# Means of squares as pairs of float32r products, some slots behind the lead group, in a two-block transformer on one core

## The chip, the core and the metric

The kernel runs on one core of one Trainium2 chip, in one launch. The metric is device time in microseconds (us): the median over executions on the chip. One execution was taken by the hardware profiler, and all rows below are from it. The engines are named as the profile names them: PE (matrix products; PEld is its loading of weights), DVE (vector), ACT (scalar functions), POOL, and SP, which here only issues transfers.

## What is computed

The input is one sequence of 512 tokens of width 1024. All arithmetic is to float32's accuracy. The first block has two layers, the second block one layer with a state space operator and one with attention:

```python
def rmsnorm(x, g):
    xf = x.astype(jnp.float32)
    y = xf * lax.rsqrt(jnp.mean(xf * xf, axis=-1, keepdims=True) + EPS)
    return (y * g.astype(jnp.float32)).astype(x.dtype)
...
    for l in range(DEPTH):
        u = rmsnorm(x, pre_mix_g[l])
        m = token_mixer(u, w_in[l], b_gate[l], q_norm_g[l], k_norm_g[l],
...
        x = x + rmsnorm(m, post_mix_g[l])
        h = rmsnorm(x, pre_ffn_g[l]) @ w_ffn_up[l]
        f = jnp.square(jax.nn.relu(h)) @ w_ffn_down[l]
        x = x + rmsnorm(f, post_ffn_g[l])
...
        h = rms_norm(x, norm_mix[layer])
        if layer < N_A_LAYERS:
            x = x + s5_mixer(h, ssm_w_in[layer], ssm_a_re[layer], ssm_a_im[layer],
...
        x = x + conv_ffn(rms_norm(x, norm_ffn[layer]), ffn_w_up[layer],
```

In `token_mixer` the product with `w_in` gives queries, keys and values of a grouped-query attention, a query and a key of lower rank (the latents; each gets an rmsnorm of its own before it is multiplied up), and gates. The change is about the means of squares inside these norms: those of the stages' inputs and those of the latents.

## The kernel before

**Layout.** Activations lie feature-major: 1024 features are 8 tiles of 128 partitions by 512 tokens. Each weight and each activation is kept as a pair of float32r parts, hi and lo, and each product is made in three float32r passes (hi by hi, hi by lo, lo by hi). In the trace such a triple is two rows `mm<-xg,wh` and one row `mm<-xg,wl`. An output tile of a product over 8 tiles of input is 24 products of 512 columns. A product of plain float32 operands is two records in the trace.

**The norm is applied late.** A stage multiplies the input, scaled by the norm's gain, with its weights at once, and the factor 1/sqrt(mean + eps) of each token is applied when an output tile leaves PSUM. So the mean of squares must be known only then. The squares are made by ACT (`sq`), summed over the 8 tiles by POOL and DVE (`acc`; in most stages the last tile's square stays apart in `sq`), and `mean_mm` sums over the partitions with one or two float32 products by a matrix of 1/n (`ones_d` in the tile `consts`). `rstd` then makes the factor `rr` with Ln, Exp and Square on ACT and two steps on DVE.

**The lead group.** A stage begins with `lead_group`: its first three or four output tiles are made input tile by input tile, so that PE can start with the first input tile. Inside a boundary between stages it does so for the two halves of the columns one after the other, while DVE and ACT make the input tiles `xg`. Behind its last product stands `pre()`, which is the mean and `rstd`, and four slots later the closures that take the group's tiles out of PSUM. There are 8 PSUM tiles.

**Order.** The program is a list of closures. `later(n, fn)` puts a closure behind n more slots of products, where a slot is 512 columns of float32r, and a float32 product of 512 columns counts as four. The scheduler of the framework then orders the instructions of each engine by its own estimate of times; `pin` keeps an instruction behind what its engine was given before. So a stage's closures can move when another closure's products count otherwise.

**The state space stage** (`ssm`). PE makes `u` tiles as any stage; DVE applies the factor (`u<-mm,rr`), and each tile goes out to DRAM (`ud`) and comes back in another order (`U`). Blocks of eight float32 products of at most 64 columns follow: `vps<-U` (the chunk's contribution to the states, copied by ACT into `VS0`, `VS1`, `VS2`, which hold tiles 0 and 1, tiles 2 to 4 and tiles 5 to 7), `yps<-U`, `yps<-VS` and `yps<-fx`. Between them DVE runs a scan over each of VS0, VS1 and VS2 (lines 1427 to 1431, five operations a step), in the order of the program. In the profile's rows the number is left out, so that VS0 and VS1 both read VS. The result, after `gq`, comes back as `yhl`, and the products `mm<-yhl` with the stage's second weight follow.

Of the kernel before, what the change touches and what calls it, by code (L numbers as in the profile page):

```python
# [107 lines left out]
class Kernel:  # L108
# [21 lines left out]
    LAG = 3  # L130
    LD = 2
# [28 lines left out]
    # ---------------------------------------------------------------- tiles  # L160
# [20 lines left out]
    # -------------------------------------------------------------- weights  # L181
# [14 lines left out]
    def split_early(self, h):  # L196
        """half of the first three units"""
        for u in self.early:
            t = self.raw[u][0]
            if h == 0:  # L200
                hi, lo = (self.pool.tile([128, 1024], F32R, name=x, tag=x, bufs=W_BUFS) for x in ("wh", "wl"))
                self.whl[u] = [hi], [lo], 1024
            c = slice(512 * h, 512 * h + 512)
            hi, lo = self.whl[u][0][0][:, c], self.whl[u][1][0][:, c]
            self.pin(self.nc.scalar.activation(hi, t[:, c], AF.Copy))
            self.nc.vector.tensor_tensor(lo, t[:, c], hi.bitcast(F32), ALU.subtract)
            if h == 1:
                self.raw.pop(u)
# [29 lines left out]
    def weight(self, u, a, m):  # L238
        """columns a .. a + m of both parts of a unit"""
# [53 lines left out]
    def later(self, n, fn):  # L293
        """emit fn once n more slots (of 512 columns) of products have been emitted"""
# [11 lines left out]
    # ------------------------------------------------------------- matmuls  # L306
# [7 lines left out]
    def pin(self, ins):  # L314
        """ins stays behind what its engine has been given so far"""
        self.tc.keep_in_program_order(ins)

    def mm_tok(self, out, x, t, u, a, first, last, n=256):
        """out [128 tokens of tile t, n] += x[:, tokens].T @ W[columns a .. a + n of a unit], in three float32r passes"""
# [14 lines left out]
    def mm3(self, ps, u, k0, nk, kt, m0, m, xs, first, last, ncol=None, cols=ALL):  # L334
        """ps += W[k-tiles, cols].T @ x over nk k-tiles, in three float32r passes."""
# [10 lines left out]
    def split(self, dst, src, scale=None, gain=None):  # L346
        """dst[:,0] + dst[:,1] = src (times scale or a per-partition gain)."""
# [14 lines left out]
    def ln(self, out, in_, load=True, **kw):  # L362
        """Ln from the table set that has Exp too; load: unless it is there already."""
# [6 lines left out]
    def rstd_a(self, v, l=None, cols=ALL, load=True):  # L370
        """v: mean square, the same in all the rows it is used for (PSUM)."""
# [8 lines left out]
    def rstd_b(self, vyq, name="r", cols=ALL, r=None, pin=False):  # L380
        """one Newton step; the result is -2 / sqrt(v + eps): y * ((v + eps) * y * y - 3)"""
# [12 lines left out]
    # ------------------------------------------------------- generic phases  # L394
    def sq_acc(self, st, src, i, n, scale=1.0, cols=ALL, pin=False, one=False):
        """running sum of squares over tiles; the last stays apart."""
# [26 lines left out]

    def lead_group(self, units, n, xs, evac, st, ones="ones_d", pre=None, mid=None, feed=None):
        """The first n output tiles k-tile by k-tile, so that the products start with the first tile of x;
        mid: the two halves of the columns one after the other, with mid() once the first has begun."""
        pss = []

        def emit(k, cols, last):
# [4 lines left out]
            if last and k == KT - 1:  # L434
                if pre is not None:
                    pre()
                    self.later(4, lambda: [evac(j, pss[j]) for j in range(n)])
# [34 lines left out]
    def half_tiles(self, units, xs, nk, evac, js, fin):  # L472
        """the last output tiles, the two halves of the columns one after the other; fin() in the second"""
# [24 lines left out]
    # ================================================================ setup  # L498
# [37 lines left out]
    def begin_norm(self, gain, xs, st):  # L536
        """split x * gain, and start the sum of squares of x: a closure for each tile."""
# [8 lines left out]
    def boundary(self, f, st, gain, nxt, res):  # L546
        """x += the norm of f; then begin_norm of the next norm; the closures for the two halves of the columns."""
# [29 lines left out]
    # ================================================================= FFN  # L577
    def ffn1(self, l, xs, st, nxt, mid, bg=None, last=(), feed=None):
# [7 lines left out]
        def pre():  # L586
            st["r"] = self.rstd(self.mean_mm(st, self.const("ones_d")), "rr", load=False)
# [55 lines left out]
    # =============================================================== mixer  # L643
# [9 lines left out]
    def head_norm(self, z, gain, then, n1, n2):  # L653
        """rms norm over the 64 rows of each head, times gain; then(result)."""
# [17 lines left out]
    def v_tiles(self, vf, vst):  # L672
        """v feature-major [two heads of 64, tokens] -> vst [token, tile, head, (hi | lo)]."""
# [8 lines left out]
    def stack(self, dst, src, scale=None):  # L682
        """src [two heads of 64, S] -> dst[h] with hi and lo stacked on the partitions."""
# [11 lines left out]
    def dup(self, dst, src, scale=None):  # L695
        """src [two heads of 64, S] -> dst[h] [128, (hi, lo), S], each on both halves of the partitions."""
# [13 lines left out]
    def softmax_ops(self, name, qk, vst, ydst, spill=None):  # L710
        """The parts of a softmax attention over 8 heads in blocks of 128 queries, by name; a block (h, qt) is 4 h + qt.
        q: scores, e: exponentials, n: division by the sum, t: transposes, p: product with the values, two blocks at once.
        qk(h, qt, ps): scores. vst(h): [128, 4, 128] (hi | lo). ydst: pairs of heads -> hi/lo tiles."""
# [69 lines left out]
    def chunks(self, unit, xs, nk, evac, j, n, m0=0, ncol=None, k0=0):  # L783
        """one output tile as n closures, for use between other work."""
# [14 lines left out]
    def mixer(self, l, xs, st, nxt, mid, feed=None):  # L799
# [6 lines left out]
        def pre():  # L806
            st["r"] = self.rstd(self.mean_mm(st, self.const("ones_d")), "rr", load=False)
# [59 lines left out]
        def ev_c(which, n):  # L867
            def f(j, ps):
# [3 lines left out]
                if j == n - 1:  # L872
                    self.later(18, mean)

            def mean():
                a = self.rstd_a(self.mean_mm(cst[which], self.const("ones_" + which)))
# [16 lines left out]
        def kr_mm():  # L893
            """the products of both parts of w_kr with hi in one pass, one below the other"""
# [26 lines left out]
        # ---- grouped-query attention  # L921
# [8 lines left out]
        # ---- latent attention operands, a pair of heads at a time  # L930
# [36 lines left out]
        def v_chunk(i, c):  # L967
            """the values of the heads of two pairs, for two tiles of tokens, token-major"""
# [16 lines left out]
        def prep(p):  # L985
# [5 lines left out]
            # column tiles of q_up: rope0 nope0 | nope1 rope1 | nope2 nope3  # L991
# [64 lines left out]
        # ---- branches, gates and output product  # L1056
# [48 lines left out]
    # ======================================================== second block  # L1105
    def exp32(self, x, n, out):
        """exp to float32's accuracy on a small tile: 2^k * polynomial."""
# [58 lines left out]
    def ssm_gen(self):  # L1166
        """The state space operators, from the parameters alone, as a list of closures:
        WT (chunk -> state), O (state -> chunk) and T (the lags inside a chunk) in DRAM.
        States have the real part on the first 64 partitions, the imaginary on the others;
        the places j of a chunk are stored from the last to the first."""  # L1170
# [33 lines left out]
        def factor():  # L1204
            """f = (a_bar - 1) / a"""
# [20 lines left out]
        def powers(R, I, n):  # L1226
            """the powers n + 1 .. 2n from 1 .. n"""
# [15 lines left out]
        def tables():  # L1243
            """P1 = re | im, P2 = -im | re of the powers 0 .. 8"""
# [7 lines left out]
        def outer():  # L1252
            """powers 1 .. 8 of a_bar^8 for the scan"""
# [13 lines left out]
        def expansion(out, c1, c2, a):  # L1267
            """out[g, d, h] = c1[g, h] * P1[a + d, g] + c2[g, h] * P2[a + d, g]; in closures"""
# [19 lines left out]
        def gen(i):  # L1288
# [10 lines left out]
            def bbar():  # L1299
                """bb = f * b"""  # L1300
# [12 lines left out]
            def stacks():  # L1313
                """bs = bb re | bb im, c = c | -c, c0 = c re | -c im"""
# [60 lines left out]
    def ssm(self, xs, st, nxt, mid, feed=None):  # L1375
# [9 lines left out]
        def pre():  # L1385
            st["r"] = self.rstd(self.mean_mm(st, self.const("ones_d")), "rr", load=False)
# [28 lines left out]
        def scan(k):  # L1415
            """states after each chunk: inside blocks of 8 chunks, from block to block, and the blocks' starts added."""
# [6 lines left out]
            def step(s, o, m, sh, temp):  # L1423
                """o += a * s, with a = m(re) and m(im | -im)"""
# [632 lines left out]
```

## Time and profile before

| what | value |
|---|---|
| device time, median of 3 runs | 2788.34 us (2786.98 to 2790.88) |
| span of the profiled execution | 2786.1 us |
| PE busy | 2722.6 us, 98% |
| DVE busy | 1846.5 us, 66% |
| ACT busy | 1305.1 us, 47% |
| POOL busy | 293.4 us, 11% |

The profiled execution's own time is its span and what lies around it; the median of the runs is 2.2 us above the span. PE is busy for nearly the whole span, so a PE instruction that is removed, or a wait of PE that is shortened, is what can be seen in the time; an instruction on another engine is seen only where PE waits for it.

### The profile page before, as it was taken

The page shows a single profiled execution, that of the slowest core. Times are in us where ns is not written, and L with a number is a line of the kernel's source. Part 1 is how long each engine was busy: PE and PEld are TensorE (multiplying, and loading weights), DVE is VectorE, ACT ScalarE, POOL GpSimd, SP SyncE. Part 2 cuts the span into 40 slices and gives each one's busy share as a digit, 9 for nine tenths or more (in the row PEclk, how much of TensorE's full clock was granted, in tenths as well). Part 3 has the DMA queues.
Part 4 walks back from the last instruction along what each step waited for, and adds up shares of the span by engine and source line. Part 5 has one row for each costly group of instructions (what it writes and reads, how often), then busy time and mean ns, then how long its engine had stood idle before and what let it go on. Part 6 is the DMA issues. An engine that isn't in the chain of part 4 may idle for free.

```text
span 2786.1 us, 35356 instructions
## 1 busy us (share of the span) xinstructions
PE 2722.6 (98%) x13470; PEld 2268.2 (81%) x13470; DVE 1846.5 (66%) x2963; ACT 1305.1 (47%) x2204; POOL 293.4 (11%) x311
## 2 busy tenths in 40 slices
PE   8999999999999999999999989999999999999998
PEld 6888888888878888888887887888887888888887
DVE  7889863444687996787745784656466667574654
ACT  6567553333465664532334214423236888542333
POOL 1000020000210101121002000101012111110101
PEclk9999999999999999999999879999999999999999
DMA  5323333333232334354445623233324223233331
GB/s 206 116 79 91 121 119 97 95 98 98 96 109 86 93 95 161 110 190 153 137 123 180 183 88 117 91 99 98 99 85 131 68 69 103 84 98 99 98 92 61
DMA packets 122651, 307.47 MB, mean 110 GB/s; under 512 B 35824, under 2 KB 42736, under 8 KB 122352
## 3 DMA queue, kind: packets, MB, share of 16 engines
q1 hardware_dynamic: 109424, 291.57, 32.7%
q10 hardware_dynamic: 10624, 8.39, 1.0%
q0 software_dynamic: 2432, 5.25, 0.9%
q8 instruction: 106, 1.74, 0.3%
q14 instruction: 65, 0.53, 0.1%
HBM read 260.59 MB, written 41.68 MB: 108 GB/s over the span
## 4 chain that ended last, share of the span: by engine, by line
PE 58%; DVE 5%; ACT 1%; issue 1%; DMA 0%; POOL 0%; SPq 0%; DVEq 0%; ACTq 0%; POOLq 0%
PE mm L312 49%; PE z L312 3%; PE yps L312 2%; PE o L312 1%; PE s L312 1%; PE vps L312 1%; DVE xg L360 0%; DVE wl L233 0%; PE gps L312 0%; PE pT L328 0%; DVE pn L567 0%; PE mean L312 0%; DVE xr L568 0%; DVE VS L1431 0%; PE gps L328 0%
## 5 line engine op out<-in xcount | busy, mean ns | idle before, releaser
L312 PE MATMUL mm<-xg,wh 128*128 128x512 f32 (+1 forms) x4080 | 1227.5, 383 | 26.6 <-DVE xg L360 15.5
L312 PEld LDWEIGHTS mm<-xg,wh 128*128 128x128 f32 x4080 | 745.4, 188 | 188.0 <-DVE xg L360 24.6
L230 ACT ACTIVATE wh<-raw 128x1024 fp32r<-128x1024 f32 (+2 forms) x417 | 431.1, 1039 | 830.0 <-PE mm L312 527.5
L312 PE MATMUL mm<-xg,wl 128*128 128x512 f32 (+1 forms) x2024 | 759.5, 378 | 0.0
L233 DVE TENSOR_TENSOR wl<-raw,wh 128x1024 fp32r<-128x1024 f32 (+2 forms) x417 | 531.3, 1278 | 161.9 <-ACT wh L230 156.7
L312 PE MATMUL mm<-hid,wh 128*128 128x512 f32 (+1 forms) x1816 | 539.1, 380 | 0.7 <-DVE hid L357 0.4
L312 PEld LDWEIGHTS mm<-xg,wl 128*128 128x128 f32 x2024 | 381.7, 189 | 71.6 <-issue 0.2
L312 PEld LDWEIGHTS mm<-hid,wh 128*128 128x128 f32 x1816 | 335.0, 188 | 67.0 <-DVE hid L357 1.2
L312 PE MATMUL mm<-hid,wl 128*128 128x512 f32 (+1 forms) x908 | 343.9, 379 | 0.0
L312 PE MATMUL mm<-yhl,wh 128*128 128x512 f32 x640 | 207.3, 403 | 8.7 <-ACT yhl L1494 4.7
L414 POOL TENSOR_TENSOR acc<-acc,sq 128x256 f32<-128x256 f32 (+1 forms) x90 | 106.6, 1185 | 953.1 <-ACT sq L402 952.5
L312 PEld LDWEIGHTS mm<-hid,wl 128*128 128x128 f32 x908 | 170.8, 188 | 31.8
L312 PEld LDWEIGHTS mm<-yhl,wh 128*128 128x128 f32 x640 | 120.1, 192 | 34.6 <-DVE yhl L1495 5.7
L1582 POOL TENSOR_TENSOR gt<-gt,cv 128x512 f32<-128x512 f32 x44 | 74.9, 1703 | 592.7 <-ACT wh L230 471.1
L312 PE MATMUL mm<-yhl,wl 128*128 128x512 f32 x320 | 127.1, 397 | 0.0
L591 DVE SCALAR_TENSOR_TENSOR ht<-mm,rr 128x512 f32<-128x512 f32 x64 | 43.8, 690 | 117.1 <-PE mm L312 116.8
L1590 DVE SCALAR_TENSOR_TENSOR xr<-mm,xr 128x512 f32<-128x512 f32 (+1 forms) x50 | 33.5, 670 | 125.3 <-PE mm L312 125.3
L607 DVE TENSOR_TENSOR part<-part,mm 128x512 f32<-128x512 f32 (+1 forms) x52 | 33.5, 644 | 113.9 <-PE mm L312 113.8
L1570 DVE SCALAR_TENSOR_TENSOR gt<-mm,rr 128x512 f32<-128x512 f32 x88 | 60.6, 690 | 69.6 <-PE mm L312 69.5
L722 DVE TENSOR_REDUCE nm<-s 128x1 f32<-128x512 f32 x128 | 86.4, 680 | 20.8 <-PE s L312 20.4
L749 ACT ACTIVATE pt<-pT 128x512 fp32r<-128x512 f32 x128 | 74.6, 594 | 46.2 <-PE pT L328 45.0
L729 ACT ACTIVATE p<-s,nm 128x512 f32<-128x512 f32 x128 | 87.1, 684 | 11.0 <-DVE nm L722 8.9
(297 smaller groups left out, 3463.5 us busy)
## 6 DMA issues: line engine op xcount, KB each, us to landing
raw<-in_w_up SPq DMA_DIRECT2D x152, 512.0 KB, 3.6
raw<-in_w_down SPq DMA_DIRECT2D x96, 512.0 KB, 3.5
raw<-in_w_in SPq DMA_DIRECT2D x51, 512.0 KB, 3.6
xd<-xr SPq DMA_DIRECT2D x16, 512.0 KB, 2.8
gd<-z SPq DMA_DIRECT2D x32, 256.0 KB, 2.2
g<-gd SPq DMA_DIRECT2D x32, 256.0 KB, 3.9
raw<-in_w_o SPq DMA_DIRECT2D x16, 512.0 KB, 3.6
raw<-in_w_glu SPq DMA_DIRECT2D x16, 512.0 KB, 4.3
```

What stands on the lines that cost most here:

```text
L230: ins = self.nc.scalar.activation(h, x, AF.Copy)
L233: ins = lo_engine.tensor_tensor(l, x, h.bitcast(F32), ALU.subtract)
L312: return self.nc.tensor.matmul(out, lhsT, rhs, **kw)
L414: eng.tensor_tensor(st["acc"][:, cols], st["acc"][:, cols], sq[:, cols], ALU.add)
L591: nc.vector.scalar_tensor_tensor(t, ps, 0.0, st["r"], op0=ALU.max, op1=ALU.mult)
L607: nc.vector.tensor_tensor(p, p, ps[:, cols], ALU.add)
L722: nc.vector.tensor_reduce(nm, ps, AX.X, ALU.max, negate=True)
L729: nc.scalar.activation(p, ps, AF.Exp, bias=nm, accum_out=sm)
L749: nc.scalar.activation(hi[:, :, q0:q0 + 128], v, AF.Copy)
L1570: v.scalar_tensor_tensor(t, ps, -0.5, st["r"], op0=ALU.mult, op1=ALU.mult)
L1582: nc.gpsimd.tensor_tensor(t, t, sg.pop(n), ALU.mult)
L1590: v.scalar_tensor_tensor(x, ps[:, cols], 0.5, x, op0=ALU.mult, op1=ALU.add)
```

## The change

In seven lead groups (both mixers, both feed-forward stages of the first block, the state space stage, both feed-forward stages of the second block) and in the four norms of latents, the float32 products of `mean_mm` are replaced. `sum_split` makes one tile of the sum on DVE where the last square lay apart, and splits it, times -1/n, in a hi and a lo part (ACT and DVE, tile `mhl`); `mean_r` multiplies both parts by a float32r matrix of -1 that was there already. In the lead groups `pre()` moves 10 slots behind the group's last product (`PRE`), and the evacuation four slots behind that. In the latents the split stands 6 slots behind the last tile and the mean 18 slots behind it, as before. The attention stage of the second block, the boundaries, the head norms and the last norm keep float32. The rest of the diff takes out comments, so that line numbers behind line 130 move by 1, those behind line 430 by up to 19.

```diff
+    PRE = 10
...
+    def sum_split(self, st, n):
+        if "sq" in st:
+            self.nc.vector.tensor_tensor(st["acc"], st["acc"], st["sq"], ALU.add)
+        st["hl"] = self.s4("mhl")
+        self.split(st["hl"], st["acc"], scale=-1.0 / n)
+
+    def mean_r(self, st):
+        v = self.ps("mean")
+        for i in range(2):
+            self.mm(v, self.ones_r, st["hl"][:, i], start=i == 0, stop=i == 1)
+        return v
...
                 if pre is not None:
-                    pre()
-                    self.later(4, lambda: [evac(j, pss[j]) for j in range(n)])
+                    self.sum_split(st, D)
+
+                    def rest():
+                        pre()
+                        self.later(4, lambda: [evac(j, pss[j]) for j in range(n)])
+                    self.later(self.PRE, rest)
...
         def pre():
-            st["r"] = self.rstd(self.mean_mm(st, self.const("ones_d")), "rr", load=False)
+            st["r"] = self.rstd(self.mean_r(st), "rr", load=False)
...
                 if j == n - 1:
+                    self.later(6, lambda: self.sum_split(cst[which], 128 * n))
                     self.later(18, mean)
...
             def mean():
-                a = self.rstd_a(self.mean_mm(cst[which], self.const("ones_" + which)))
+                a = self.rstd_a(self.mean_r(cst[which]))
```

How the instructions move is not to be read from the diff. On PE, at the end of the first mixer's lead group (the first stage of the program), the order before is this; `xg` is the input, `wh` and `wl` the parts of the weights:

```order
L312 MATMUL mm<-xg,wl 128x512
L312 MATMUL mean<-acc,consts 128x512
L312 MATMUL mean<-sq,consts 128x512
L312 MATMUL mm<-xg,wh 128x512 x2
L312 MATMUL mm<-xg,wl 128x512
```

And with the change, from the same last product of the group on:

```order
L313 MATMUL mm<-xg,wl 128x512
L313 MATMUL mm<-xg,wh 128x512 x2
L313 MATMUL mm<-xg,wl 128x512
L313 MATMUL mm<-xg,wh 128x512 x2
L313 MATMUL mm<-xg,wl 128x512
L313 MATMUL mm<-xg,wh 128x512 x2
L313 MATMUL mm<-xg,wl 128x512
L313 MATMUL mm<-xg,wh 128x512 x2
L313 MATMUL mm<-xg,wl 128x512
L313 MATMUL mean<-mhl,ones_r 128x512 x2
L313 MATMUL mm<-xg,wh 128x512 x2
```

The mean stands 12 products later, since it is emitted between closures of 12 products, and is two float32r products instead of two float32 ones.

On PE in the state space stage, before the first products with the scanned states, the order before is:

```order
L312 MATMUL mm<-xg,wl 128x512
L312 MATMUL vps<-U,wt 128x64 x16
L312 MATMUL mm<-xg,wh 128x512 x2
L312 MATMUL mm<-xg,wl 128x512
L312 MATMUL mm<-xg,wh 128x512 x2
L312 MATMUL mm<-xg,wl 128x512
L312 MATMUL mm<-xg,wh 128x512 x2
L312 MATMUL mm<-xg,wl 128x512
L312 MATMUL yps<-VS_14466,ot 128x63 x8
L312 MATMUL vps<-U,wt 128x64 x8
L312 MATMUL yps<-fx,ot 128x7x7 x8
```

With the change it is as follows (VS_14466 before and VS_14502 here are both VS0):

```order
L313 MATMUL mm<-xg,wl 128x512
L313 MATMUL mm<-xg,wh 128x512 x2
L313 MATMUL mm<-xg,wl 128x512
L313 MATMUL yps<-VS_14502,ot 128x63
L313 MATMUL vps<-U,wt 128x64 x16
L313 MATMUL yps<-VS_14502,ot 128x63 x7
L313 MATMUL vps<-U,wt 128x64 x8
L313 MATMUL yps<-fx,ot 128x7x7 x8
```

The two blocks `vps<-U` of tiles 3 and 4, 16 products, stood ahead of the first product that needs the scanned VS0, and now stand behind it. From there on PE's order is the same as before to the end of the stage.

On DVE in the same stage, from the last input tile to the third `u`, the order before is:

```order
L360 SCALAR_TENSOR_TENSOR xg<-xr_13746,cols,xg 128x256 x2
L233 TENSOR_TENSOR wl<-raw,wh 128x1024 x2
L384 SCALAR_TENSOR_TENSOR rl<-mean,rl 128x512
L388 SCALAR_TENSOR_TENSOR rr<-rl,ry 128x512
L1390 SCALAR_TENSOR_TENSOR u<-mm,rr 128x512
L233 TENSOR_TENSOR wl<-raw,wh 128x1024
L1390 SCALAR_TENSOR_TENSOR u<-mm,rr 128x512
```

With the change:

```order
L361 SCALAR_TENSOR_TENSOR xg<-xr_13778,cols,xg 128x256 x2
L428 TENSOR_TENSOR acc<-acc,sq 128x512
L355 SCALAR_TENSOR_TENSOR mhl<-acc,mhl 128x512
L234 TENSOR_TENSOR wl<-raw,wh 128x1024 x3
L385 SCALAR_TENSOR_TENSOR rl<-mean,rl 128x512
L389 SCALAR_TENSOR_TENSOR rr<-rl,ry 128x512
L1409 SCALAR_TENSOR_TENSOR u<-mm,rr 128x512
```

Two operations of the split have come in, and a third weight (`wl`, which waits for ACT's `wh`) stands ahead of the chain that makes `rr`.

## Rows read from the trace of the kernel before

**Rows 1.** The page: span; busy time, share and instructions of PE.

```profile
span 2786.1 us, 35356 instructions
PE 2722.6 (98%) x13470; PEld 2268.2 (81%) x13470; DVE 1846.5 (66%) x2963; ACT 1305.1 (47%) x2204; POOL 293.4 (11%) x311
```

**Rows 2.** Timeline of PE, end of the lead group of the first feed-forward stage.

```profile
410.68 1.02 PE L312 MATMUL mean<-acc,consts 128*128 128x512 f32 x2
411.53 1.02 PE L312 MATMUL mean<-sq,consts 128*128 128x512 f32 x2
...
412.86 0.40 PE L312 MATMUL mm<-xg,wl 128*128 128x512 f32 x1
413.09 0.40 PE L312 MATMUL mm<-xg,wh 128*128 128x512 f32 x1
```

**Rows 3.** Timeline of PE, the first mean of a latent.

```profile
150.66 1.02 PE L312 MATMUL mean<-acc,consts 128*128 128x512 f32 x2
...
151.99 0.39 PE L312 MATMUL mm<-xg,wl 128*128 128x512 f32 x1
```

**Rows 4.** Timelines of DVE and ACT at the lead end of rows 2.

```profile
410.76 3.50 DVE L233 TENSOR_TENSOR wl<-raw,wh 128x1024 fp32r<-128x1024 f32 x3 [2.49 <-ACT wh L230]
...
409.67 2.95 ACT L230 ACTIVATE wh<-raw 128x1024 fp32r<-128x1024 f32 x3 [1.82 <-PE mm L312]
```

**Rows 5.** Instructions of lines 356 and 357: duration in ns, min/median/max.

```profile
L356 ACT ACTIVATE hid<-gt x44: 632/632/635, 1779.9 to 2742.2; 128x512 fp32r<-128x512 f32 x44
L357 DVE TENSOR_TENSOR hid<-gt,hid x44: 676/684/694, 1781.1 to 2742.8; 128x512 fp32r<-128x512 f32 x44
```

**Rows 6.** Timeline of PE inside the same lead group; in brackets the idle time before.

```profile
402.79 0.38 PE L312 MATMUL mm<-xg,wh 128*128 128x256 f32 x1 [0.81 <-DVE xg L360]
```

**Rows 7.** Timelines of PE and DVE, second mixer: its first scores.

```profile
809.94 1.16 PE L312 MATMUL s<-kk,qs 128*128 128x512 f32 x2 [5.26 <-DVE qs L693]
810.90 1.91 PE L312 MATMUL mean<-sq,consts 128*128 128x512 f32 x2
...
809.20 1.41 DVE L693 SCALAR_TENSOR_TENSOR qs<-qro,qs 64x512 fp32r<-64x512 f32 x2
```

**Rows 8.** Timeline of PE in the state space stage.

```profile
1577.97 3.76 PE L312 MATMUL vps<-U,wt 128*128 128x64 f32 x32 [0.67 <-DVE u L1390]
...
1587.07 2.60 PE L312 MATMUL yps<-VS,ot 128*128 128x63 f32 x16 [3.22 <-DVE VS L1431]
1589.46 3.62 PE L312 MATMUL vps<-U,wt 128*128 128x64 f32 x16
1592.88 3.60 PE L312 MATMUL yps<-fx,ot 128*128 128x49 f32 x16
...
1620.15 1.20 PE L312 MATMUL mm<-yhl,wh 128*128 128x512 f32 x2
...
1624.03 1.89 PE L312 MATMUL yps<-U,tt 128*128 128x64 f32 x16
1625.76 1.95 PE L312 MATMUL yps<-VS,ot 128*128 128x63 f32 x16
```

**Rows 9.** A stretch of that stage: length, busy time (count) of PE, PEld, DVE, ACT and POOL, granted clock, DMA share, GB/s.

```profile
1588.00:1622.00 34.00, 34.00 (x158) 33.62 (x158) 31.91 (x84) 8.56 (x13) 0.00 (x0) 0.50 0.48 150
```

**Rows 10.** Timeline of DVE in that stage.

```profile
1561.08 0.40 DVE L1427 TENSOR_TENSOR t<-VS,SI 64x128 f32<-64x128 f32 x1 [5.45 <-ACT VS L1404]
1562.97 1.13 DVE L1390 SCALAR_TENSOR_TENSOR u<-mm,rr 128x512 f32<-128x512 f32 x1
1564.02 1.21 DVE L233 TENSOR_TENSOR wl<-raw,wh 128x1024 fp32r<-128x1024 f32 x1
...
1586.83 0.19 DVE L1431 TENSOR_TENSOR VS<-VS,t0i 128x16 f32<-128x16 f32 x1
...
1590.42 0.49 DVE L1427 TENSOR_TENSOR t<-VS,SI 64x192 f32<-64x192 f32 x1
...
1630.38 0.69 DVE L1480 SCALAR_TENSOR_TENSOR gq<-gq,yps 128x512 f32<-128x512 f32 x1 [3.39 <-ACT gq L1479]
```

More of the change, by code (lines that the diff above doesn't have):

```diff
@@ L806, in pre @@
         def pre():
-            st["r"] = self.rstd(self.mean_mm(st, self.const("ones_d")), "rr", load=False)
+            st["r"] = self.rstd(self.mean_r(st), "rr", load=False)
         def scaled(ps, rows=128):
@@ L1385, in pre @@
         def pre():
-            st["r"] = self.rstd(self.mean_mm(st, self.const("ones_d")), "rr", load=False)
+            st["r"] = self.rstd(self.mean_r(st), "rr", load=False)
         def ev_u(i, ps):
@@ L1564, in pre @@
         def pre():
-            st["r"] = self.rstd(self.mean_mm(st, self.const("ones_d")), "rr")
+            st["r"] = self.rstd(self.mean_r(st), "rr")
         def up(j, ps):
```

## The prediction

> **What bounds the kernel.** I read the page first: PE is busy 98% of the span [rows 1], so the sum is made on PE, and another engine counts only where PE waits for it. Then I looked up every mean that is replaced in PE's timeline. PE enters each without a wait, straight behind the group's products, so before the change a mean costs its full PE time. Two things remain to be found from the order: which waits of PE the later `rr` makes, and what else moves. For that I went through all waits of PE above 0.2 us, and read the stretches with the largest ones on DVE too. Two stretches matter. In the second mixer PE waits 5.26 us for the queries of the first scores [rows 7]. In the state space stage PE waits 3.22 us for the end of the scan over VS0, and then runs a long row of small products at a granted clock of 0.50, the lower level of 1.2 GHz, while it is busy all the time [rows 8, 9].
>
> **The products that go.** At a lead group with `acc` and `sq`, four float32 records and the two float32r products behind them take 412.86 - 410.68 = 2.18 us, and one float32r product takes 413.09 - 412.86 = 0.23 [rows 2]. So two float32 products take 2.18 - 0.46 = 1.72, and the two float32r products that come instead 0.46: 1.26 saved. Five groups are of this kind (both mixers, both first feed-forward stages, the state space stage): 6.3 us. Where only `acc` was there, one float32 product takes 151.99 - 150.66 - 0.46 = 0.87 [rows 3], so 0.41 is saved, six times (four latents, two second-block feed-forward stages): 2.5 us. All of it together is 8.8 us, 0.3% of the time, if nothing else happened.
>
> **What is added.** Eleven splits of 128x512: an ACT copy (0.63 by the nearest row) and a DVE operation (0.68), and in five groups one DVE addition more (0.68 by the same row, of the same shape) [rows 5]. At a lead group's end they cost nothing: there DVE had been idle 2.49 us and ACT 1.82 before their next weights [rows 4], which covers 1.36 and 0.63, and 12 products of 0.23, 2.7 us, stand between the split and the mean. If that cover were gone, the weights' splits would come some 1.4 us later; with four weights held ahead that still reaches PE only in part, so I keep 0 to +0.5 a group as its bound, and take 0. `rr` is ready later by the 12 products (2.7) less the 1.7 of the old mean, so about 1.0 later. The evacuation four slots behind it moves by as much; the group's four tiles, the mean and the next tiles have eight PSUM tiles, and at 24 x 0.23 = 5.5 us a tile there is room for two tiles more before a product needs one that is still full.
>
> **Matmuls that move into waits.** In three lead groups with two halves PE waits 0.81 or 0.82 for the fourth input tile of the second half [rows 6]; the other two are alike. With the change the scheduler puts two products of the next tile there, which fill 0.45 of it. That is a further 0.45 in the first two feed-forward stages, and in the second mixer.
>
> **Sum outside the state space stage.** First mixer 1.26 (its first scores do not wait for queries, but the slack is small: bounds 0 and 1.26); the two feed-forward stages of the first block 2 x (1.26 + 0.45) = 3.4; four latents 1.6; two second-block feed-forward stages 0.8. In the second mixer PE reaches the first scores about 1.2 earlier, but waits there for DVE's `qs`, the last of a chain in which DVE is not idle [rows 7], and which begins with tiles that are taken out about 1.0 later. I let the scores start 1.2 later, since the order on DVE has one more pair of operations ahead of `qs` and one weight less. Against that one float32 head mean of 0.86, which stood right behind the scores [rows 7], now runs ahead of the wait, inside it. Net +0.3, bounds -1.5 and +2. Together: -1.3 - 3.4 - 1.6 - 0.8 + 0.3 = **-6.8 us**, bounds about -8.5 and -4.
>
> **The state space stage.** Its lead group ends when DVE has made the last input tile, so nothing is saved in the group. DVE's order then has the split and a third weight ahead of the chain to `rr`. The third weight costs 1.21 [rows 10] more and the mean's place 1.0, of which the idle time ahead takes part: I let the first `u` come 1.5 later and the scan over VS0 start 1.8 later, at 1562.9 instead of 1561.08 [rows 10] (bounds 0, since the scan waited 5.45 for ACT's copy of `vps`, which other orders can bring earlier, and +4, if the second `U`, which now stands behind a transfer of a weight in SP's queue, comes late). The scan itself took 1587.02 - 1561.08 = 25.9. In it stood four `u` of 1.13 and two `wl` of 1.21, 6.9 together [rows 10]; with the change three `u` and one `wl` stand there, 4.6. So it ends at 1562.9 + 25.9 - 2.3 = 1586.5, half a microsecond earlier than before (bounds 1584.5 and 1588.5).
>
> The price is in what stands behind that end. Before, the blocks `vps<-U` of tiles 3 and 4 were done at 1577.97, at full speed, 3.76 for both, ahead of the wait [rows 8]. Now they stand behind the first product with VS0, and PE runs its queue in order, so it waits with nothing to do for some 3 us more, and then has two blocks more to do. In that place a block takes 1592.88 - 1589.46 = 3.42, and the row of blocks begins with one that took only 2.39 since the clock had not yet fallen [rows 8]. The wait is now about as long as the 5.26 of the second mixer. Behind that one the clock was low at once: two products of 512 columns took 0.96, against 0.46 [rows 7, 2]. So I take 3.4 for the first block too, +1.0. From VS0's end to the first `mm<-yhl` it was 1620.15 - 1587.07 = 33.1; it becomes 33.1 + 1.0 + 2 x 3.42 = 40.9, and `mm<-yhl` starts at 1586.5 + 40.9 = 1627.4, **7.3 us later**. DVE is busy 31.91 of the 34 us [rows 9], and its scan over VS1 needs the two blocks, so it starts about 4 us later than 1590.42. But it must wait for PE's `yps` anyway before it goes on to `gq`, and behind 1626 it waits 3.39 for PE [rows 10]. So PE sets the pace, and the delay is handed on to the end of the stage. Bounds +3 (the clock falls no sooner than before and the scan ends at 1584.5, with one wait behind it that takes up part) and +10.
>
> A rule of the Trainium skill speaks against this step. TensorE: Matmul & The Clock Gate, in the section What's actually happening, says that the default state is throttled and that activity releases the throttle. By it the row of blocks, which keeps PE busy, would bring the clock back, and the two blocks would cost 1.8 each and not 3.4. The trace does not agree here: PE was busy 34.00 of 34.00 us and the clock stayed at 0.50 [rows 9]. By the rule the delay would be some 3 us smaller or turn into a gain; that is rival A.
>
> **Sum.** -6.8 + 7.3 = +0.5 us. The profiled span of 2786.1 becomes 2786.6; with the 2.2 by which the median of the runs lies above the span this is 2788.8, and I take **2789 us**. One part in 500, 5.6 us, is about what a measurement can tell from no change, and the likeliest case's own range, 2783 to 2795, is that.
>
> **Rivals.** A: the clock comes back in the row of blocks. If it does after three of them, eight blocks cost 1.8 in place of 3.42, 13 us less; the stage gains 6, and the time is 2789 - 13 = 2776. For it speaks that the moved products change when PE works; against it the 34 us in which it did not come back. Chance 0.10.
>
> B: the delay is taken up behind the stage's blocks, since PE waits again there for `yhl` and DVE's third scan; or the scan ends early enough that half the delay is gone. Then the stage costs 0 to 2 and the savings show: 2788.3 - 6.8 + 1 = 2782.5. Against it stands that DVE itself waits for PE at 1630.38 [rows 10]. Chance 0.18; half of it would show as faster.
>
> C, the other side: the clock does not come back at `mm<-yhl`. Before, a row of 512-column products from 1620.15 to 1624.03 stood between the slow blocks and the next ones, and the block at 1624.03 took 1.73 [rows 8]. If with a longer slow stretch the clock has not risen when that row ends, the next eight blocks, which took about 1.8, take 3.4: 8 x 1.6 = 13 us, and the time is 2802. It decides whether the block behind `mm<-yhl` takes 1.7 or 3.4. Chance 0.12. A fourth possibility, that the second mixer's wait grows by more than I let it and the scan starts 4 late (+2 and +3, 2794), lies inside the likeliest case or just above it: 0.10 for what is above.
>
> **Chances.** The likeliest case 0.50, A 0.10, B 0.18, C 0.12, the fourth 0.10. Faster by over 0.2% are A, half of B and 0.06 of the tail of the likeliest: 0.25. Slower are C, most of the fourth and 0.03 of the tail: 0.22. Within 0.2% 0.53. The range goes from 2779 to 2800, which leaves out A and C.
>
> **What would show it.** Two `mean<-mhl` rows of 0.23 behind 12 products in each group, with no wait; waits of 0.4 in place of 0.8 at the fourth tile; the first scores of the second mixer about 7.5 us behind an idle PE; in the state space stage a wait of 5 to 6 us before `yps<-VS`, then two blocks `vps<-U` of 3.4 each, and the first `mm<-yhl` 40 us behind the end of the wait. The forecast is wrong if these blocks run at 1.8, if PE waits for a tile of PSUM or a weight behind the lead groups, or if the waits at the scores or at the blocks are of another size.

## The result, and the profile after

The changed kernel takes 2813.95 us (2812.42 to 2815.08, 4 runs) against 2788.16 before (4 runs): ratio 1.0088, 95% interval 1.0075 to 1.0100. It is slower by 26 us where I forecast no change, and lies above my range. The page after, with span and PE's busy time:

```profile
span 2812.7 us, 35353 instructions
PE 2729.8 (97%) x13460; PEld 2280.2 (81%) x13460; DVE 1855.8 (66%) x2979; ACT 1309.6 (47%) x2213; POOL 298.5 (11%) x311
```

PE issues ten records fewer and is busy 7 us longer than before [rows 1], though the change takes 8.8 us of products away by the forecast, so part of the loss is PE at its lower clock; the rest of the 26.6 us by which the span grew, 19.5, is waiting. To find the places I took the same product in both traces, stage by stage, and subtracted the starts. The last column says where the shift stands at the end of each place:

| place | forecast, us | measured, us | shift after it |
|---|---|---|---|
| start, first mixer's lead group | -1.3 | -1.4 | +0.4 to -1.0 |
| its latents | -0.8 | **+8.3** | +7.3 |
| first feed-forward stage | -1.7 | -0.6 | +6.7 |
| second mixer's lead group and first scores | +0.3 | +1.7 | +8.4 |
| its latents | -0.8 | **+7.5** | +15.9 |
| second feed-forward stage | -1.7 | -1.7 | +14.2 |
| state space stage | +7.3 | **+13.5** | +27.7 |
| second block's feed-forward stages | -0.8 | -0.9 | +26.8 |

**Where it went as forecast.** Timeline of PE after, behind the lead group of the first feed-forward stage, and the second mixer's first scores:

```profile
420.43 0.63 PE L313 MATMUL mean<-mhl,ones_r 128*128 128x512 f32 x2
420.89 0.62 PE L313 MATMUL mm<-xg,wh 128*128 128x512 f32 x2
...
818.42 1.22 PE L313 MATMUL s<-kk,qs 128*128 128x512 f32 x2 [7.67 <-DVE qs L711]
```

The two products of the mean take 0.46 together and wait for nothing, in place of 1.72 [rows 2]. The lead group of this stage, with the waits filled, gave 1.6 of the 1.7 forecast; the boundary behind the stage took 1.0 back. The wait at the scores is 7.67, where 7.5 was forecast, in place of 5.26 [rows 7].

**The latents.** Timeline of PE at the second latent of the first mixer, before:

```profile
176.75 0.63 PE L312 MATMUL s<-kk,qs 128*128 128x512 f32 x2
177.22 1.02 PE L312 MATMUL mean<-acc,consts 128*128 128x512 f32 x2
177.67 1.03 PE L312 MATMUL s<-kk,qs 128*128 128x512 f32 x2
...
181.75 0.62 PE L312 MATMUL mm<-xg,wh 128*128 128x512 f32 x2
```

And after, with ACT's and DVE's rows there:

```profile
176.22 1.11 PE L313 MATMUL o<-pt,vst 128*128 128x256 f32 x8
182.79 1.59 PE L313 MATMUL mean<-mhl,ones_r 128*128 128x512 f32 x2 [5.46 <-ACT mhl L354]
184.18 1.05 PE L313 MATMUL s<-kk,qs 128*128 128x512 f32 x2
...
189.01 0.71 PE L313 MATMUL mm<-xg,wh 128*128 128x512 f32 x2
```

```profile
178.31 1.28 ACT L367 ACT_TABLE_LOAD   x1
181.59 0.63 ACT L357 ACTIVATE krhl<-krr 32x512 fp32r<-32x512 f32 x1 [2.00 <-DVE krr L669]
182.12 0.61 ACT L354 ACTIVATE mhl<-acc 128x512 fp32r<-128x512 f32 x1
...
180.88 0.68 DVE L669 TENSOR_TENSOR krr<-rp,sh 32x512 f32<-32x512 f32 x1
182.86 0.67 DVE L355 SCALAR_TENSOR_TENSOR mhl<-acc,mhl 128x512 fp32r<-128x512 f32 x1
```

DVE's last addition to `acc`, before and after, and PE's weight loads for the mean's two products, after:

```profile
175.40 0.68 DVE L414 TENSOR_TENSOR acc<-acc,sq 128x512 f32<-128x512 f32 x1
...
174.40 0.68 DVE L415 TENSOR_TENSOR acc<-acc,sq 128x512 f32<-128x512 f32 x1
...
182.79 0.29 PEld L313 LDWEIGHTS mean<-mhl,ones_r 128*128 128x128 f32 x1 [5.66 <-ACT mhl L354]
183.58 0.29 PEld L313 LDWEIGHTS mean<-mhl,ones_r 128*128 128x128 f32 x1 [0.51 <-DVE mhl L355]
```

The sum `acc` was ready at 176.1 before and is at 175.1 now. Before, PE read it directly. Now ACT has to split it, and in ACT's queue the split stands behind `krhl`, the rotary key's own split, which waits for a chain of DVE. ACT is at work ahead of `krhl` until 179.6 too, so by estimate about 2.5 of the wait are `krhl`'s and the rest is what stands before it. The next scores, transposes and products stand behind the mean in PE's order, and all of them wait 5.46 us with it. The two float32r products then take 1.39 in place of 0.46: the second also waits for DVE's part of the split, until 183.58. From 182.79 to 189.01 PE's granted clock is 0.51, the lower level; behind that it is 1.00 again. The second layer's row is the same to the hundredth: 938.16, a wait of 5.46.

**The state space stage.** PE's first two blocks before, then PE, DVE's start of the scan, SP's queue and the longest wait of the weight `wt` in it, all after:

```profile
1555.05 1.89 PE L312 MATMUL vps<-U,wt 128*128 128x64 f32 x16
1558.45 1.97 PE L312 MATMUL vps<-U,wt 128*128 128x64 f32 x16 [1.23 <-issue]
```

```profile
1571.20 3.66 PE L313 MATMUL vps<-U,wt 128*128 128x64 f32 x16 [3.95 <-DMA U<-ud]
...
1579.18 3.65 PE L313 MATMUL vps<-U,wt 128*128 128x64 f32 x16 [3.36 <-DVE u L1409]
...
1607.24 0.69 PE L313 MATMUL yps<-VS,ot 128*128 128x63 f32 x2 [6.96 <-DVE VS L1450]
1607.72 7.04 PE L313 MATMUL vps<-U,wt 128*128 128x64 f32 x32
1614.55 3.19 PE L313 MATMUL yps<-VS,ot 128*128 128x63 f32 x14
...
1648.22 1.20 PE L313 MATMUL mm<-yhl,wh 128*128 128x512 f32 x2
...
1653.35 1.89 PE L313 MATMUL yps<-U,tt 128*128 128x64 f32 x16
1655.08 1.95 PE L313 MATMUL yps<-VS,ot 128*128 128x63 f32 x16
...
1583.48 0.38 DVE L1446 TENSOR_TENSOR t<-VS,SI 64x128 f32<-64x128 f32 x1 [4.76 <-ACT VS L1423]
```

```profile
1568.46 0.32 SPq L1413 DMA_DIRECT2D U<-ud  x1
1568.87 0.38 SPq L194 DMA_DIRECT2D raw<-in_w_glu  x1
1574.89 0.32 SPq L1390 DMA_DIRECT2D wt<-wd  x1
1575.31 0.38 SPq L1413 DMA_DIRECT2D U<-ud  x1
...
SPq L1390 <- PE vps L313: 5.6, 1, 5.6
```

The two blocks behind the start of `yps<-VS` take 1614.55 - 1607.72 = 6.83 us, at the lower clock, as forecast. From the end of the wait to `mm<-yhl` it is 1648.22 - 1607.24 = 40.98 (forecast 40.9, before 33.1 [rows 8]). What I missed lies ahead: the second block `vps<-U` starts 8 us behind the first, where it was 3.4 before, because the second `U` is issued at 1575.31, behind a weight that waits 5.6 us for the first block on PE (1574.89). Measured from the stage's last input tile, which DVE makes 14.2 later than before, the first block starts 1.9 later, the second another 4.6 later, and the second takes 3.4 in place of 1.8, since PE had waited 3.95 and 3.36 ahead of the two and ran both at the lower clock (granted 0.53 and 0.50). So the scan over VS0 starts 8.2 later, at 1583.48, where I had 1.8. It then takes 2.2 less than before (forecast 2.3), and PE goes on with VS0 20.2 us later [rows 8]: 5.9 more than the 14.2, where I had 0.5 less.

The stretch of the blocks, with the columns of [rows 9]:

```profile
1607.00:1648.00 41.00, 40.76 (x191) 40.76 (x192) 32.39 (x83) 7.51 (x12) 0.00 (x0) 0.50 0.44 134
```

### The profile page after: what moved, and what is told of

It is laid out like the page before. It is cut to its first block, busy times and chain, and to the rows that moved or that the text cites. A ratio compares the mean times of both kernels' runs of the same rounds, so it can differ in the third digit from the quotient of the medians.

```text
span 2812.7 us, 35353 instructions
## 1 busy us (share of the span) xinstructions
PE 2729.8 (97%) x13460; PEld 2280.2 (81%) x13460; DVE 1855.8 (66%) x2979; ACT 1309.6 (47%) x2213; POOL 298.5 (11%) x311
## 4 chain that ended last, share of the span: by engine, by line
PE 57%; DVE 5%; ACT 1%; DMA 1%; issue 1%; POOL 0%; SPq 0%; DVEq 0%; ACTq 0%; POOLq 0%
PE mm L313 49%; PE z L313 3%; PE yps L313 2%; PE o L313 1%; PE vps L313 1%; PE s L313 1%; DVE xg L361 1%; DVE wl L234 0%; PE gps L313 0%; DVE pn L585 0%; PE pT L329 0%; DVE xr L586 0%; DVE VS L1450 0%; PE gps L329 0%; PE mean L313 0%
## 5 line engine op out<-in xcount | busy, mean ns | idle before, releaser
L768 DVE TENSOR_TENSOR pt<-pT,pt 128x512 fp32r<-128x512 f32 x128 | 86.7, 684 | 12.4 <-ACT pt L767 11.5
```

The source lines that it names most:

```text
L768: nc.vector.tensor_tensor(lo[:, :, q0:q0 + 128], v, hi[:, :, q0:q0 + 128].bitcast(F32), ALU.subtract)
```

## The experiments

All ran on one chip per group of four, beside the kernel before (2790.14 for e1 to e4, 2789.7 for e5 to e8, 2789.59 for e9 to e12). Each ratio is to the kernel before, with its 95% interval.

### e1 to e4: the latents and the stage, apart and together

e1 gives the four latents their float32 means back:

```diff
-                    self.later(6, lambda: self.sum_split(cst[which], 128 * n))
                     self.later(18, mean)
...
-                a = self.rstd_a(self.mean_r(cst[which]))
+                a = self.rstd_a(self.mean_mm(cst[which], self.const("ones_" + which)))
```

> The changed kernel, with the four latents' means as float32 products again (no split there). Theory 1 (what the trace of the changed kernel shows): at the second latent of each mixer PE waits 5.46 us for ACT's part of the split, which stands in ACT's queue behind an operation (krhl) that waits for DVE, and runs at the lower clock behind it; each layer loses 8.3 us there. Without the split both waits are gone: 2814 - 2 x 8.3 + 2 x 0.4 (the float32 product costs more) + 2 x 0.4 (the first latent) = 2799. Rival: the latents' wait only stands in for a wait for the same DVE chain a little later, so that PE waits for krhl's user or the next scores instead: 2808 to 2814.

Measured: 2798.41 us, ratio 1.0029 (1.0017 to 1.0041). e2 gives only the state space stage its old lead group back:

```diff
-                if pre is not None:
+                if pre is not None and not pair:
+                    pre()
+                    self.later(4, lambda: [evac(j, pss[j]) for j in range(n)])
+                elif pre is not None:
                     self.sum_split(st, D)
...
-            st["r"] = self.rstd(self.mean_r(st), "rr", load=False)
+            st["r"] = self.rstd(self.mean_mm(st, self.const("ones_d")), "rr", load=False)
```

(`pair` is False for this stage alone.)

> The changed kernel, with the state space stage's lead group as before (float32 mean directly behind the group, evacuation 4 slots later). Theory 1: the stage lost 14 to 15 us to the changed order (late U tiles, long wait for VS0, two blocks behind it at the lower clock) and gets it back: 2814 - 14.5 = 2799.5, between 2798 and 2801. Rival (my prediction's size): only about 7 us are lost to the order there and the rest to something that stands before the stage: 2807.

Measured: 2801.13, ratio 1.0037 (1.0023 to 1.0051). e3 is both edits:

> The changed kernel, with both the latents and the state space stage's lead group as before; the pairs remain in both mixers' lead groups and in the four feed-forward stages. Theory 1: the two losses are independent and add up, 2814 - 15 - 14.5 = 2784.5, some 3.5 us under the kernel before, since the lead groups save 1.25 to 1.7 each but the second mixer gives some 3 back at its first scores. Rival: the losses are one (PE late by the latents meets other DMA traffic in the stage), and together give no more than the larger one alone: 2799.

Measured: 2787.87, ratio 0.9994 (0.9985 to 1.0002). The losses are two, and they add up as nearly as the intervals tell: by the ratios 16.5 and 14 apart, 26 together. It ends 3 us above what I expected of it, no faster than before by the interval. e4 leaves the latents' pairs and moves their split to the front:

```diff
-                    self.later(6, lambda: self.sum_split(cst[which], 128 * n))
+                    self.sum_split(cst[which], 128 * n)
                     self.later(18, mean)
```

> The changed kernel, with the latents' split made right behind the last tile's square instead of 6 slots later; the mean stays 18 slots behind. In ACT's queue the split then stands ahead of krhl. Theory 1: the place in ACT's queue alone makes the wait, so both waits go and the pairs' savings stay: 2814 - 2 x 8.3 = 2797.5. Rival: the split itself is too much for ACT and DVE between the attention's operations, so that PE waits there in any place: within 4 us of 2814.

Measured: 2797.97, ratio 1.0030 (1.0018 to 1.0042), as good as no split at all. Its timelines at the place of the 5.46 us:

```profile
175.39 0.63 ACT L354 ACTIVATE mhl<-acc 128x512 fp32r<-128x512 f32 x1 [1.44 <-DVE acc L415]
...
176.48 0.39 PE L313 MATMUL mean<-mhl,ones_r 128*128 128x512 f32 x1
176.71 0.40 PE L313 MATMUL s<-kk,qs 128*128 128x512 f32 x1
```

The same operations on the same engines, only with the split ahead of `krhl` in ACT's queue: ready in time, and PE doesn't wait. It was the place, not the work. (In e4 the split stands ahead of more rows of ACT than `krhl` alone, so the run doesn't show the share of each.)

### e5 to e7: what the stage lost by

All three start from e4. e5 makes the stage's mean with float32 products, 10 slots late as in the change:

```diff
-                    self.sum_split(st, D)
+                    if pair:
+                        self.sum_split(st, D)
...
-            st["r"] = self.rstd(self.mean_r(st), "rr", load=False)
+            st["r"] = self.rstd(self.mean_mm(st, self.const("ones_d")), "rr", load=False)
```

(`pair` is again False for this stage alone.)

> The kernel with the latents' split at once (e4), and in the state space stage a float32 mean without a split, but still 10 slots behind the lead group. On PE the two blocks vps<-U of tiles 3 and 4 then stand ahead of the first product with VS0 again; in SP's queue the second U still stands behind the transfer wt<-wd4, which waits for the first block vps. The trace of e4 puts the stage's loss at 12.5 us: 4.5 because VS0 ends later, 7.8 for the two blocks and the first one at the lower clock. Theory 1: the blocks' part goes and the other stays: 2798 - 7.8 = 2790. Rival (the blocks are all, since VS0's end only matters with them behind it): 2785.5. Rival (the place of the blocks does nothing, the low clock would come anyway): 2798.

Measured: 2791.11, ratio 1.0008 (0.9999 to 1.0017); 6 us under e4 by the ratios. PE's timeline in e5:

```profile
1583.35 6.82 PE L313 MATMUL vps<-U,wt 128*128 128x64 f32 x32 [4.15 <-DVE VS L1451]
1589.96 3.62 PE L313 MATMUL yps<-VS,ot 128*128 128x63 f32 x16
```

The blocks take 6.8 here too, at the lower clock. But they lie beside VS0's scan, which ends at 1588.6, and PE's wait is 4.15 in place of 6.96. e6 keeps the pair and makes its mean at once (`PRE` is 0 for this stage):

```diff
-                    self.later(self.PRE, rest)
+                    self.later(self.PRE if slots is None else slots, rest)
```

> The kernel with the latents' split at once (e4), and in the state space stage the pair's mean directly behind the lead group instead of 10 slots later. PE's order has the two blocks ahead of the wait again, SP's order still has wt<-wd4 ahead of the second U. PE waits for the split at the lead group's end (a DVE addition, an ACT copy and a DVE operation, 0.68 + 0.63 + 0.69, so about 2 us). Theory 1: the blocks' 7.8 go, the first u comes some 2 us earlier, and the wait of 2 us is new but lies ahead of a wait for VS0 that PE has anyway: 2798 - 7.8 - 1 = 2789. Rival (what costs in the stage is the pair, its three operations ahead of rr, not the order): 2796.

Measured: 2792.27, ratio 1.0013 (1.0004 to 1.0022), 5 us under e4 and halfway between what the two theories gave, so it doesn't decide between them. By the traces the stage, from its last input tile to the products behind its last wait for `yhl`, takes 12.2 more than before in e4, 8.9 in e6 and 5.0 in e5. In e6 the first `u` comes 0.7 later than in e4, not 2 earlier, and VS0 ends no earlier than in the change: only the blocks' part went. So some 4 us between e6 and e5 may be the pair's operations; the medians, 1 us apart, don't show it. e7 takes the weights out of the way of the second `U`:

```diff
-    LDQ = 'sync'
+    LDQ = 'gpsimd'
```

> The kernel with the latents' split at once (e4), and the stage's operators (wt, tt) loaded through POOL's queue instead of SP's, all else as changed. The second U then doesn't stand behind wt<-wd4, and on PE the two blocks stand ahead of most of the products with VS0. Theory 1 (VS0 ends late because the second U waits in SP's queue for the first block vps): both parts of the loss go but for the 2 us by which rr is later: 2798 - 12.5 + 2 = 2787.5. Rival (VS0 ends late because u is late and its way through DRAM is slow, whatever SP's order): 2798 - 7.8 = 2790 or more.

Measured: 2779.3 (2773.42 to 2787.37), ratio 0.9966 (0.9954 to 0.9979), 8 us better than I expected. The trace is that of its shortest execution. The second block comes 3.0 us behind the first again, and PE's timeline and the stretch of the blocks show the rest:

```profile
1550.26 1.97 PE L313 MATMUL vps<-U,wt 128*128 128x64 f32 x16 [1.48 <-DMA U<-ud]
1553.28 1.97 PE L313 MATMUL vps<-U,wt 128*128 128x64 f32 x16 [0.54 <-DMA U<-ud]
...
1576.47 3.75 PE L313 MATMUL vps<-U,wt 128*128 128x64 f32 x32 [0.81 <-DMA U<-ud]
1581.51 1.00 PE L313 MATMUL yps<-VS,ot 128*128 128x63 f32 x8
...
1596.04 3.74 PE L313 MATMUL vps<-U,wt 128*128 128x64 f32 x32
```

```profile
1580.00:1600.00 20.00, 19.66 (x168) 19.15 (x167) 19.36 (x41) 6.11 (x9) 0.00 (x0) 1.00 0.46 128
```

PE has no wait for VS0 ahead of the row of blocks, and the whole row runs at the full clock: two blocks in 3.75 where they took 7. Neither theory had that.

### e8 to e12: the best parts, and controls

e8 starts from e4 and gives the stage and the second mixer their old lead groups back; the diff is e2's, for the mixer under `l == 1` as well:

> The pairs only where they should pay: latents (split at once), the first mixer, and the four feed-forward stages; the state space stage's and the second mixer's lead groups as before. Theory 1: each place keeps what its own instructions give, by the hand sums 1.25 + 2 x 1.7 + 4 x 0.4 + 2 x 0.4 = 7.0 with nothing lost: 7 us under the kernel before (0.25%). By the trace of e4, in which the first mixer gave 0.7, its latents 0.9 and the first feed-forward stage 0.6, it is less: 4.5 to 5 us under it, ratio 0.998. Rival: the saved PE time is taken up by the next wait of each stage: no change, ratio 1.000.

Measured: 2782.44, ratio 0.9975 (0.9965 to 0.9984). Both the hand sum of 7 us and the 4.5 to 5 read from e4's trace lie within the interval (4.5 to 10 us), which doesn't tell them apart. e12 is e8 with the pair in the second mixer:

> e8 with the pair in the second mixer's lead group, as in the changed kernel. Theory 1: PE's wait for queries there grows by more than the pair saves, as in the trace of the changed kernel (7.66 us in place of 5.26): e8's 2782.4 + 1.6 = 2784. My prediction had +0.3 for that group and with it 2781.5, since without the pair the group would be as before.

Measured: 2786.47, ratio 0.9986 (0.9977 to 0.9995). The first scores in e8 and in e12:

```profile
806.59 1.22 PE L313 MATMUL s<-kk,qs 128*128 128x512 f32 x2 [5.33 <-DVE qs L714]
```

```profile
808.40 1.22 PE L313 MATMUL s<-kk,qs 128*128 128x512 f32 x2 [7.65 <-DVE qs L714]
```

They start 1.8 later with the pair, but a float32 head mean that stands behind them in e8 has then already run, and the shift between the two traces is 0.1 us some 3 us later. So between these two traces the pair costs about what I forecast (+0.3). The +1.7 of the table is then mostly not the pair's: e8, without it, loses 1.3 in the same place against the kernel before. The 4 us between the medians of e8 and e12 are no more than the two intervals allow, so the size stays open.

e9, e10 and e11 ask what made e7 fast. The edit is e7's one line, in the kernel before (e9), in e4 with the second mixer's old lead group (e10), and in e8 (e11):

> The control for e7: the kernel before, unchanged but that the stage's operators (wt, tt) are loaded through POOL's queue. In e7 PE had no long wait ahead of the row of small blocks, the row began at a clock of 1.00 and stayed there for 18 us, with 1.7 us a block in place of 3.4. Theory 1 (e7's gain is that the row begins with the high clock, and the late rr with more products between the blocks is what took the wait away): the kernel before keeps its wait of 3.2 us for VS0 and its low clock, so 2786 to 2791. Rival (the queue alone makes U, VS0 and the row earlier, whatever the mean): 2772 to 2778.

Measured: 2789.49, ratio 0.9998 (0.9989 to 1.0007).

> e7 with the second mixer's lead group as before. By the traces the pair costs 1.3 to 2 us at the second mixer's first scores. Theory 1: 2779.3 - 1.6 = 2777.7. Rival (the second mixer's wait for queries ends at the same DVE operation either way): 2779.3 or more.

Measured: 2780.83 (2776.68 to 2786.83), ratio 0.9970 (0.9958 to 0.9981), not told apart from e7.

> e8 with the stage's operators loaded through POOL's queue; the stage's mean is float32 and at once. It stands to e10 as the early mean to the late one. Theory 1 (with the early mean PE waits for VS0 and the row of blocks runs at the low clock): as e8, 2780 to 2784. Rival (the queue alone brings the gain): 2768 to 2772.

Measured: 2782.88, ratio 0.9974 (0.9964 to 0.9985), as e8. So the queue alone gives nothing; of the means tried with it, only the late pair makes it pay. The same row of blocks in e9:

```profile
1591.23 3.67 PE L312 MATMUL yps<-VS,ot 128*128 128x63 f32 x16 [2.48 <-DVE VS L1431]
```

```profile
1591.00:1622.00 31.00, 30.77 (x145) 30.77 (x145) 29.49 (x78) 6.83 (x11) 0.00 (x0) 0.50 0.48 148
```

PE waits for VS0 (2.48; 2.02 shortly ahead of it are for a `U`), and the row runs at 0.50 for its whole length. Which of the late pair's moves took that wait away in e7 (the products left between the blocks, or the later `rr`) no run here separates. The fastest version measured is e7, with e10 beside it; e10's trace is that of its longest execution, and there too the row runs at 1.00 (1581.50 to 1599.80).

## Why the prediction was wrong

**Right:** the price of the products (0.46 for 1.72), the filled waits in the lead groups, the second mixer's wait (7.67 for 7.5), the two blocks that moved behind the wait, their 3.4 each, the 40.9 us to `mm<-yhl`, the 2.2 by which the scan got shorter, and that the delay is handed on: 13.8 at the first `mm<-yhl`, 13.5 at the end of the stage. Of the rivals, A (the clock comes back in the row) did not happen: the row ran 41 us at 0.50. Nor did B, since the delay was not taken up, nor C: the block behind `mm<-yhl` took 1655.08 - 1653.35 = 1.73. Of the fourth possibility the late start of the scan came, at 8.2 where it had 4.

**The step that failed first** is "Eleven splits of 128x512 ... At a lead group's end they cost nothing". I found the cover at the lead groups and let it stand for the latents too, which I entered as a saving of 1.6 us. There the splits stand among the attention's operations, with other rows ahead of them in ACT's queue. The term was +15.8 and not -1.6; e1 and e4 take it away, e4 by the place of the split alone. For these four I had not asked what stands ahead of the split there; the excerpts of the order show the lead groups and the stage, and not the latents.

**The second** is the end of the scan over VS0, "half a microsecond earlier than before". I named the cause, the second `U` behind a weight in SP's queue, but as the far bound (+4) of a start that I took 1.8 late. The weight cannot be issued before the first block `vps` has finished on PE, so the second `U` could not be early: the place in the queue made a chain (first block, weight, second `U`, second block), and the chain, not an estimate between bounds, gives the number. The start came 8.2 late: 1.9 with the first block, 4.6 by the chain (about 1.7 of it, by estimate, since the first block too ran at the lower clock), and 1.6 since the second block ran at the lower clock behind a wait that I did not have. So VS0 ended 5.9 later, and PE waited 6.96 for it where I had 5 to 6. In e7, where the chain is cut, the second block is back at 3.0 us behind the first.

Together, 15.8 + 1.6 = 17.4 for the latents and 13.5 - 7.3 = 6.2 for the stage, these make 24 of the 26 us by which I was off. The boundary behind the first feed-forward stage, which took back 1.0, and the second mixer, 1.4 over the forecast, make the rest.

The Trainium skill's TensorE: Matmul & The Clock Gate, section HAM oscillation — how this bites in real kernels, advises to keep PE free of long idle gaps because the clock falls in them. The trace agrees at the second latent of the first mixer: 5.46 us of idle time, and a granted clock of 0.51 in the 6.2 us behind it. In the section What's actually happening it says that activity releases the throttle; the row of blocks does not agree, with 40.76 us of PE busy in 41.00 at 0.50.

## What to carry to other kernels

When a step is taken off PE by giving work to other engines, look for each of its places in those engines' queues, one by one: what stands ahead of the new operation there, and what that waits for. A copy of 0.63 us behind an operation that waits for another engine cost 8 us a layer, and nothing where it stood ahead of that operation and of the rows before it. A transfer that waits for a buffer in a queue with transfers on the critical path makes a chain; follow the chain to a number and don't put it among the bounds.

## What the runs showed of the hardware

A row of some ten blocks of eight float32 products of at most 64 columns ran at either clock: 18 us at 1.00 in e7, 31 us at 0.50 in e9, 41 us at 0.50 in the changed kernel, with PE busy nearly all the time in each. In none of these did the clock come back within the row. In the kernel before it fell in the row's first block, which took 2.39, and the next took 3.42 [rows 8]. At the start of each row at 0.50 PE had waited, from 2.31 (e11) to 7.16 us (e4), and at the start of those at 1.00 (e7 and e10) at most 0.81. No run varied this wait alone, so that it decides is argued and not shown.

Later in the stage no such difference is to be seen. e7 and e10 wait alike there (3.32, 2.54, 1.35 and 0.98 us; 3.09, 2.56, 1.17 and 0.96) and then run the same six blocks, whose granted clocks are, e7 first:

```profile
1646.00:1662.00 16.00, 14.56 (x112) 13.24 (x110) 11.29 (x30) 5.32 (x9) 0.00 (x0) 1.00 0.16 50
```

```profile
1650.00:1675.00 25.00, 24.22 (x108) 22.54 (x109) 10.56 (x25) 6.00 (x11) 0.00 (x0) 0.55 0.16 47
```

Between these two traces the shift grows by 9.6 us there; what made the clock fall in e10 stays open. It may be why e7's and e10's single times spread over 14 and 10 us, where the kernel before spreads over 7: in e7 the mean granted clock is 0.993 in the shortest execution and 0.986 in the longest. Only one execution of each has a trace, so the place isn't shown.
